# Three of the four pieces of each MLP down product as Strassen's seven half-size products, in a decoder kernel on one core

## The chip, the cores and the metric

The kernel runs on one core of a Trainium2 chip. The metric is the device time of one execution in microseconds; several runs of the same kernel are given by their median. The engines are TensorE (PE, with its weight loads as PEld), VectorE (DVE), ScalarE (ACT), GpSimd (POOL) and SyncE (SP, which issues most of the transfers).

## The reference

Two decoder blocks on 512 tokens of 1024 features, all in float32. The first block has two layers, each an attention (latent, then sliding window), a layer norm, an MLP and another layer norm; the second block is a convolution with a dilated attention, a gated feed-forward and an embedding branch. The change is in the MLPs of the first block:

```
def _mlp(x, w_up, w_down):
    h = jax.nn.relu(x @ w_up)          # [512, 1024] @ [1024, 4096]
    return (h * h) @ w_down            # [512, 4096] @ [4096, 1024]

x = _layernorm(alpha * x + _mlp(x, mlp_w_up[l], mlp_w_down[l]), ln_mlp_g[l], ln_mlp_b[l])
```

## The kernel before

A float32 product is made of three products of exact parts. `split` (L115) makes them: ScalarE casts the source to the high part, VectorE subtracts it from the source to get the low part. `mm3` (L197) then issues high x high, high x low and low x high into one accumulation. Weights come in chunks of 128 x 1024 values through `wchunk` (L151): SP loads one into a raw slot (three of them, tile names wr), and the split writes a pair of slots wh and wl, four pairs in all (pool `wp`, L53). Large tiles of 128 x 2048 values, among them the transposed activations (xth, xtl), come from thirteen slots (`bp`, L54). Eight PSUM banks of 128 x 512 hold accumulations.

Names in the rows: `wl<-wr,wh` is the low part of weights, `hh` and `hl` are the parts of the squared activations with the features on partitions, `fm`, `tm`, `tt` and `up` are banks of products, `x` is the residual stream with tokens on partitions.

`mlp_ln` (L883) is called once in each of the two layers. `up(gr)` makes 512 of the 4096 hidden features: four banks, 96 mm3 steps of three matmuls over the eight row blocks of the weights; its `ev` takes Relu on ScalarE (L896), the square on VectorE (L897) and the split. `rows(ga)` takes two groups, 1024 hidden features, for one piece of the down product. `gemm_tm` (L348) does a piece for all four token blocks and for one half of the 1024 output columns after the other, and `ev_add` (L874) adds each bank to x. The order is written out by hand:

```
            for gr in range(4):
                up(gr)
            gemm_tm(*rows(0), [LO, HI], ev_add(x, ALPHA))
            up(4), up(5)
            gemm_tm(*rows(2), [LO, HI], ev_add(x, 1.0))
            up(6), up(7)
```

After that come the third piece and the fourth, whose second column half is done token block by token block with the layer norm (`ev_add_ln`, L809). The order on each engine is set by a scheduler from the order of the program text and from priorities: `tc.high_priority(offset=...)` moves the splits of weights ahead of other work of their engine by 60 places of program order (`W_PRIO`). On the engine the instructions then run strictly in that order.

Of the kernel before, what the change touches and what calls it, by code (L numbers as in the profile page):

```python
# [37 lines left out]
# pieces of other products between the steps of an attention loop  # L38
# [6 lines left out]
MLA_WO_AT = (0, 0, 21, 23)  # the steps that the first weights of the output projection wait for  # L45
# [3 lines left out]
def tile_hybrid_decoder(ctx: ExitStack, tc: tile.TileContext, io: dict, out: bass.AP):  # L49
# [75 lines left out]
    class Ahead:  # L125
        """The first weights of the next phase, split before this one ends."""
# [5 lines left out]
        def all(self):  # L132
            """All of them, in a pool of their own."""
            p = self.stack.enter_context(pool(f"pre{n_big[0]}", 4, "right"))
            for sp in self.specs:
                self.chunks.append(wchunk(*sp[:3], p=p, gain=(sp + (None,))[3]))
            return self

        def one(self):
            """The next one, two to a pair of large slots."""  # L140
            i = len(self.chunks)
            if i % 2 == 0:
                self.slots = [big(n).rearrange("p a c -> p (a c)") for n in ("awh", "awl")]
            dst = [t[:, i % 2 * 1024:i % 2 * 1024 + 1024] for t in self.slots]
            self.chunks.append(wchunk(*self.specs[i][:3], dst=dst))
# [5 lines left out]
    def wchunk(parts, a, b, perm=None, p=None, gain=None, dst=None, prio=W_PRIO):  # L151
        """gain: the vec column of the first of the chunk's factors along the rows."""
# [50 lines left out]
    # two heads of 64 features on the halves of the partitions: of head c the first part stands on its own half,  # L203
    # the second on the other one
# [43 lines left out]
    def fm_load(W, c0, n, K, kc=None, perm=None, gain=None):  # L248
        """The k-chunks of columns c0..c0+n: a list of (k0, kn, hi, lo)."""
# [50 lines left out]
    def half_k(pb, W, X, hf):  # L300
        """One bank of features on partitions, half of the tokens; W: the weights by rows."""
# [23 lines left out]
    def parts_m(pb, chunks, X, m):  # L325
        """one_m in steps of a chunk."""
# [7 lines left out]
    def parts_t(pb, chunks, X, t):  # L334
        """one_t in steps of a chunk."""
# [52 lines left out]
    def gemm_tm_t(X, W, groups, evac, g0=0, src=None, ahead=None, nxt=None, ch=None, mid=None):  # L388
        """The same, one token block after the other with the whole of the weights at hand."""
# [26 lines left out]
    def rsqrt(v_in, n, scale, eps):  # L416
        """(scale * v_in + eps)^-1/2: with v four times the base, s = v^-1/2 and a Newton step (3 - v s^2) s."""
# [19 lines left out]
    def put_t(xt, src, t):  # L437
        """Transposes the [128 tokens, 1024] src into token block t of xt."""
# [11 lines left out]
    class Norm:  # L450
        """Layer norm of x [128, NB, D] by token blocks: the sums come with what is added to x."""
# [27 lines left out]
    def rms_norm(x, t, g, xt, xns):  # L479
        """xt block t = transpose of x * rsqrt(mean(x^2) + eps) * g."""  # L480
# [11 lines left out]
    def scale_rows(eng, a, f):  # L492
        """a times the factor f of its row."""
# [5 lines left out]
    def tri(tl, qb):  # L499
        """Columns of query block qb for the key blocks up to it, in a packed triangle."""  # L500
# [7 lines left out]
    # the T5 bias by distance, one row per token of a block, kept in DRAM for a skewed read;  # L508
    # and the vectors along the features, one column each
# [47 lines left out]
    # ================= block 1, layer 0: latent attention ==========================  # L557
# [23 lines left out]
    with ExitStack() as mla:  # L581
# [20 lines left out]
        def v_piece(h0, t):  # L602
            """Values of four heads, tokens on partitions."""
# [205 lines left out]
    def ev_add_ln(x, alpha, g, b, after):  # L809
        """x = layer_norm(alpha * x + bank) as the column halves of a token block come in."""  # L810
# [72 lines left out]
    def mlp_ln(xt_in, x, l, first, nxt, rms=False):  # L883
        """x = layer_norm(alpha * x + mlp(x)); first: the first weights; nxt() takes those of the next phase."""
# [3 lines left out]
        def up(gr):  # L888
            hh, hl = big("hh"), big("hl")
            H[gr] = [(hh[:, m, :], hl[:, m, :]) for m in range(4)]  # L890

            def ev(gi, m, pb):
                n_big[0] += 1
                r = rt.tile([P, S], F32, tag="r", name=f"r_{n_big[0]}")
                v = rt.tile([P, S], F32, tag="v", name=f"v_{n_big[0]}")
                nc.scalar.activation(r, pb, AF.Relu)  # L896
                nc.vector.tensor_tensor(out=v, in0=r, in1=r, op=ALU.mult)  # L897
                split(hh[:, m, :], hl[:, m, :], v)

            gemm_fm(xt_in[2], wu, [(gr * 512, 512)], ev, ahead=first if gr == 0 else None)  # L900
# [34 lines left out]
    # ================= block 1, layer 1: sliding window attention ==================  # L935
# [56 lines left out]
    with swa:  # L992
# [92 lines left out]
        def pair(j):  # L1085
            """Two heads of the same kv head; for c = 1 the second of them stands first."""
# [4 lines left out]
        def wo_chunk(ks, c0):  # L1091
            """The rows of two pairs of heads, as pair() has them."""
# [71 lines left out]
    def conv3(y, u, wi, nm, m, bi):  # L1164
        """y = causal depthwise convolution of u along the tokens."""
# [8 lines left out]
    # ================= block 2: convolution and dilated attention ==================  # L1174
# [5 lines left out]
    def row_sums(sq):  # L1180
        """The sums over the features of sq [128, S]: column t for the tokens of block t."""
# [99 lines left out]
    # the three dilations as one causal softmax whose weights count the branches that see a key  # L1281
# [211 lines left out]
        # embedding branch  # L1493
# [44 lines left out]
def _constants():  # L1538
    """Tables that depend on the shapes alone."""
# [47 lines left out]
```

## Time and profile before

| | us |
|---|---|
| three runs | 1753.97, 1748.44, 1754.33 |
| their median | 1753.97 |
| profiled execution, span from first to last instruction | 1746.6 |
| profiled execution, its own device time | not given beside the span |
| PE busy | 1716.4 |
| DVE busy | 924.3 |
| ACT busy | 721.0 |

The span is that of one profiled execution on the same kernel. Busy times are sums over the instructions' spans with overlap counted once. Matmuls overlap one another, so the mean duration of one in a group is longer than the time from one to the next. The two MLPs lie at about 220 to 560 us and 743 to 1072 us of the span.

### The profile page before, as it was taken

To read this page: it belongs to the slowest core of one execution; us is meant where nothing else is said; L and a number is where in the kernel's file an instruction comes from. 1 tells how busy PE (TensorE), PEld (TensorE's weight loads), DVE (VectorE), ACT (ScalarE), POOL (GpSimd) and SP (SyncE) were. 2 spreads that over 40 slices of the span, in tenths; PEclk is the share of its full clock that TensorE was granted. 3 is DMA by queue.
4 is the path that set the end of the run, shared out by engine and by line. 5 is a ranking of instruction groups with operands and counts; after the bars stand their busy time and mean duration, and the time that the engine had idled before them with its cause. 6 is when DMAs were issued, how large, how long until landed. Compare 5 with 4: busy or idle time off the path is not lost.

```text
span 1746.6 us, 21505 instructions
## 1 busy us (share of the span) xinstructions
PE 1716.4 (98%) x8431; PEld 1423.2 (81%) x8431; DVE 924.3 (53%) x1786; ACT 721.0 (41%) x1311; POOL 8.0 (0%) x10
## 2 busy tenths in 40 slices
PE   8699999999999999999999999999999999999999
PEld 8577898888888877798888888888779888888887
DVE  5576654434344678744344435755866444443454
ACT  4366433222222568534232323544864332232342
POOL 0000000000000000000000000001000000000000
PEclk9899999999999999999999999999999999999999
DMA  5712312222333223222222233132331333333221
GB/s 183 111 56 95 123 62 97 97 97 97 99 119 106 97 67 108 68 73 96 97 97 97 96 121 121 49 109 84 100 106 50 98 97 97 99 121 96 91 97 61
DMA packets 113752, 167.59 MB, mean 96 GB/s; under 512 B 9049, under 2 KB 55410, under 8 KB 113650
## 3 DMA queue, kind: packets, MB, share of 16 engines
q1 hardware_dynamic: 104736, 150.03, 26.9%
q10 hardware_dynamic: 8914, 16.18, 3.9%
q8 instruction: 66, 1.08, 0.3%
q14 instruction: 36, 0.29, 0.1%
HBM read 160.95 MB, written 5.24 MB: 95 GB/s over the span
## 4 chain that ended last, share of the span: by engine, by line
PE 93%; DVE 2%; DMA 2%; ACT 2%; ACTq 1%; issue 0%; SPq 0%; DVEq 0%
PE tm L199 9%; PE tm L201 9%; PE tm L200 9%; PE fm L200 8%; PE fm L199 8%; PE fm L201 8%; PE tt L200 3%; PE tt L201 3%; PE tt L199 3%; PE gt L200 2%; PE up L200 2%; PE up L199 2%; PE gt L201 2%; PE gt L199 2%; PE up L201 2%; PE wo L199 2%
## 5 line engine op out<-in xcount | busy, mean ns | idle before, releaser
L117 DVE TENSOR_TENSOR wl<-wr,wh 128x1024 fp32r<-128x1024 f32 (+5 forms) x283 | 301.8, 1076 | 513.4 <-ACT wh L116 512.2
L116 ACT CAST wh<-wr 128x1024 fp32r<-128x1024 f32 (+5 forms) x283 | 261.0, 933 | 572.5 <-PE tm L201 303.7
L199 PE MATMUL fm<-xth,wh 128*128 128x512 f32 (+1 forms) x640 | 235.7, 368 | 0.2 <-ACT xth L116 0.2
L200 PE MATMUL fm<-xtl,wh 128*128 128x512 f32 (+1 forms) x640 | 235.3, 368 | 0.0
L201 PE MATMUL fm<-xth,wl 128*128 128x512 f32 (+1 forms) x640 | 235.2, 367 | 0.0
L199 PE MATMUL tm<-wh,hh 128*128 128x512 f32 x448 | 174.3, 389 | 0.0
L200 PE MATMUL tm<-wl,hh 128*128 128x512 f32 x448 | 174.3, 389 | 0.0
L201 PE MATMUL tm<-wh,hl 128*128 128x512 f32 x448 | 174.3, 389 | 0.0
L199 PEld LDWEIGHTS fm<-xth,wh 128*128 128x128 f32 x640 | 120.4, 188 | 20.3 <-ACT xth L116 0.5
L201 PEld LDWEIGHTS fm<-xth,wl 128*128 128x128 f32 x640 | 120.4, 188 | 20.0
L200 PEld LDWEIGHTS fm<-xtl,wh 128*128 128x128 f32 x640 | 120.4, 188 | 19.9
L201 PEld LDWEIGHTS tm<-wh,hl 128*128 128x128 f32 x448 | 84.1, 188 | 17.5
L199 PEld LDWEIGHTS tm<-wh,hh 128*128 128x128 f32 x448 | 84.1, 188 | 17.4
L200 PEld LDWEIGHTS tm<-wl,hh 128*128 128x128 f32 x448 | 84.1, 188 | 17.4
L199 PE MATMUL gt<-xth,wh 128*128 128x512 f32 x160 | 62.3, 389 | 0.0
L200 PE MATMUL gt<-xtl,wh 128*128 128x512 f32 x160 | 62.3, 389 | 0.0
L201 PE MATMUL up<-xth,wl 128*128 128x512 f32 x160 | 62.2, 389 | 0.0
L201 PE MATMUL gt<-xth,wl 128*128 128x512 f32 x160 | 62.2, 389 | 0.0
L199 PE MATMUL up<-xth,wh 128*128 128x512 f32 x160 | 62.2, 389 | 0.0
L200 PE MATMUL up<-xtl,wh 128*128 128x512 f32 x160 | 62.2, 389 | 0.0
L199 PE MATMUL tm<-wh,ah 128*128 128x512 f32 x152 | 59.1, 389 | 0.0
L200 PE MATMUL tm<-wl,ah 128*128 128x512 f32 x152 | 59.1, 389 | 0.0
(404 smaller groups left out, 3373.7 us busy)
## 6 DMA issues: line engine op xcount, KB each, us to landing
wr<-in_mlp_w_up_dram SPq DMA_DIRECT2D x64, 512.0 KB, 3.4
wr<-in_mlp_w_down_dram SPq DMA_DIRECT2D x64, 512.0 KB, 3.8
wr<-in_w_in_dram SPq DMA_DIRECT2D x24, 512.0 KB, 5.0
wr<-in_w_gate_dram SPq DMA_DIRECT2D x22, 512.0 KB, 3.8
wr<-in_w_up_dram SPq DMA_DIRECT2D x22, 512.0 KB, 3.5
wr<-in_w_down_dram SPq DMA_DIRECT2D x22, 512.0 KB, 3.8
wr<-in_mla_w_o_dram SPq DMA_DIRECT2D x8, 512.0 KB, 3.8
wr<-in_swa_w_q_dram SPq DMA_DIRECT2D x8, 512.0 KB, 3.9
```

The source lines that it names most:

```text
L116: turned["hi"] = nc.scalar.copy(out=hi, in_=src).ins
L117: return nc.vector.tensor_tensor(out=lo, in0=src, in1=hi.bitcast(F32), op=ALU.subtract)
L199: nc.tensor.matmul(o, lhsT=sh, rhs=mh, start=start, stop=False, skip_group_check=True)
L200: nc.tensor.matmul(o, lhsT=sh, rhs=ml, start=False, stop=False, skip_group_check=True)
L201: nc.tensor.matmul(o, lhsT=sl, rhs=mh, start=False, stop=stop, skip_group_check=True)
```

## The change

Of each layer's four down pieces the first three become one level of Strassen's scheme in Winograd's form. With A the 512 tokens x 1024 hidden features of a piece, cut in halves of 256 tokens and 512 features, and B its 1024 x 1024 weights, cut in halves of 512 rows and 512 columns, seven products of half size replace the eight. Their operands are sums and differences of the quarters, made on VectorE in place, before the split in high and low parts. A product has four row blocks, two token blocks and 512 columns: 24 matmuls. Three pairs of banks (R1, R2, R3, tile names r) take part of the products on top of each other, and each state of a pair is added to one or more quarters of x: 18 adds of 128 x 512 for a piece where there were 8.

The squared activations of these pieces are not split as they come; they are kept in float32 in two large tiles (hr), and the square is done on ScalarE. The weights of B are loaded whole, four blocks of 512 x 512 in slots of 1 MB of their own (pool `mb`, names wq); their splits go through the same four pairs wh and wl. The operands of A (names aop, high and low part in one tile) come from the thirteen large slots. The up products go in pairs of banks (256 features) instead of four. `WEAVE` sets the order of the seven steps (-1) and of the four up pairs (0 to 3) of the next two groups within a piece. The last piece and the layer norm stay as they were; other lines of the diff only lose comments.

```diff
+WEAVE = (-1, -1, -1, 0, -1, 1, -1, -1, 2, -1, 3)
+A_PRIO, B_PRIO = 120, 80
...
+        def squared(put):
+            def ev(m, pb):
...
                 nc.scalar.activation(r, pb, AF.Relu)
-                nc.vector.tensor_tensor(out=v, in0=r, in1=r, op=ALU.mult)
-                split(hh[:, m, :], hl[:, m, :], v)
-
-            gemm_fm(xt_in[2], wu, [(gr * 512, 512)], ev, ahead=first if gr == 0 else None)
+                put(m, r)
+            return ev
+
+        def put_raw(raw):
+            return lambda m, r: nc.scalar.activation(raw[:, m, :], r, AF.Square)
...
+        def down_steps(c, alpha):
...
+            for r, h in ((0, 0), (1, 1), (0, 1), (1, 0)):
+                B[r, h] = q = mb.tile([P, 4, S], F32, tag="q", name=f"wq_{n_big[0]}")
+                for i in range(2):
+                    nc.sync.dma_start(out=q[:, 2 * i:2 * i + 2, :],
+                                      in_=krows(wd, c * 8 + r * 4 + 2 * i, 2, h * 512, 512))
...
+            def product(R, a, b, start):
+                for i, (wh, wl) in enumerate(b):
+                    for tb in range(2):
+                        for k in range(2):
+                            ts_ = slice(tb * P, (tb + 1) * P)
+                            kk = 2 * i + k
+                            mm3(R[tb], (a[:, 0, kk, ts_], a[:, 1, kk, ts_]), (wh[:, k, :], wl[:, k, :]),
+                                start and kk == 0, kk == 3)
...
+            a22 = a_op(A22)
+            a_sum(A22, A22, A21, ALU.subtract)
+            s2 = a_op(A22)
+            b_sum(B11, B12, B11, ALU.add)
+            b = b_op(B11)
+            R2 = banks2("r")
+            product(R2, s2, b, True)
+            add(R2, 1, 0)
+            yield
+            a12 = a_op(A12)
+            b = b_op(B21)
+            product(R1, a12, b, False)
+            add(R1, 0, 0, alpha)
+            yield
...
+            a_sum(A12, A12, A22, ALU.subtract)
+            s4 = a_op(A12)
+            b = b_op(B22)
+            product(R2, s4, b, False)
+            add(R2, 0, 1)
+            yield
...
-            for gr in range(4):
-                up(gr)
-            gemm_tm(*rows(0), [LO, HI], ev_add(x, ALPHA))
-            up(4), up(5)
-            gemm_tm(*rows(2), [LO, HI], ev_add(x, 1.0))
-            up(6), up(7)
+            with pool("mb", 4) as mb:
...
+                for c in range(3):
+                    ds = down_steps(c, ALPHA if c == 0 else 1.0)
+                    for what in WEAVE:
+                        if what < 0:
+                            next(ds)
+                            continue
+                        gr, half = 2 * c + 2 + what // 2, what % 2
...
+                        up_pair(gr, half, ev)
-        gemm_tm(*rows(4), [LO, HI], ev_add(x, 1.0))
```

In the change's order the first place is VectorE between the third and the fourth of the seven steps, in the second piece of the first layer. Before, in a down piece, VectorE had splits of weights and runs of four adds:

```order
L117 TENSOR_TENSOR wl_537_3213<-wr_537_3211,wh_537_3212 128x1024
L877 SCALAR_TENSOR_TENSOR x1_375_1795<-x1_375_1795,tm_523_3019 128x512
L877 SCALAR_TENSOR_TENSOR x1_375_1795<-x1_375_1795,tm_524_3020 128x512
L877 SCALAR_TENSOR_TENSOR x1_375_1795<-x1_375_1795,tm_525_3021 128x512
L877 SCALAR_TENSOR_TENSOR x1_375_1795<-x1_375_1795,tm_526_3022 128x512
L117 TENSOR_TENSOR wl_538_3243<-wr_538_3241,wh_538_3242 128x1024
L117 TENSOR_TENSOR wl_545_3283<-wr_545_3281,wh_545_3282 128x1024
```

Now, at that place (aop_577 is the operand A12 of the fourth step, wl_582 the weights of the up pair after it, r_568 and r_569 the banks of the third step):

```order
L120 TENSOR_TENSOR wl_578_3478<-wq_553_3272,wh_578_3477 128x1024
L880 SCALAR_TENSOR_TENSOR x1_375_1795<-x1_375_1795,r_568_3377 128x512
L120 TENSOR_TENSOR wl_579_3482<-wq_553_3272,wh_579_3481 128x1024
L880 SCALAR_TENSOR_TENSOR x1_375_1795<-x1_375_1795,r_569_3378 128x512
L950 TENSOR_TENSOR hr_513_2838<-hr_513_2838,hr_534_3088 128x4x256
L956 TENSOR_TENSOR wq_553_3272<-wq_553_3272,wq_550_3263 128x1024 x2
L956 TENSOR_TENSOR wq_550_3263<-wq_551_3266,wq_550_3263 128x1024 x2
L120 TENSOR_TENSOR wl_582_3515<-wr_582_3513,wh_582_3514 128x1024
L120 TENSOR_TENSOR aop_577_3474<-hr_534_3088,aop_577_3474 128x1024
L120 TENSOR_TENSOR aop_586_3580<-hr_513_2838,aop_586_3580 128x1024
```

Five wide sums and a split of up weights stand ahead of the low part of A12 that the fourth step reads.

The second place is ScalarE at the same step. Before, in a down piece, it had casts of weights only:

```order
L116 CAST wh_535_3152<-wr_535_3151 128x1024
L116 CAST wh_536_3182<-wr_536_3181 128x1024
L116 CAST wh_537_3212<-wr_537_3211 128x1024
L116 CAST wh_538_3242<-wr_538_3241 128x1024
L116 CAST wh_545_3282<-wr_545_3281 128x1024
```

Now, with up_571 and up_572 the two banks of the up pair before the fourth step:

```order
L119 CAST wh_582_3514<-wr_582_3513 128x1024
L896 ACTIVATE r_575_3468<-up_571_3406 128x512
L901 ACTIVATE hr_570_3405<-r_575_3468 128x512
L119 CAST aop_577_3474<-hr_534_3088 128x1024
L119 CAST aop_586_3580<-hr_513_2838 128x1024
L119 CAST wh_583_3544<-wr_583_3543 128x1024
L896 ACTIVATE r_576_3471<-up_572_3407 128x512
```

The cast of A12 stands behind the Relu and the square of the up pair's first bank.

The third place is VectorE in the layer norm that ends the second layer's attention, just ahead of the second MLP (names nm, rv, rr, ra, ro are 128x1 values of the norm, gb its gain and bias). Before:

```order
L460 SCALAR_TENSOR_TENSOR x1_375_1795,sum_943_6396<-x1_375_1795,tt_944_6398 128x512
L423 SCALAR_TENSOR_TENSOR ra_940_6375<-rv_937_6372,rs_939_6374 128x1
L427 SCALAR_TENSOR_TENSOR ro_941_6376<-ra_940_6375,rs_939_6374 128x1
L466 TENSOR_SCALAR nm_945_6412<-sum_943_6396 128x1
L472 SCALAR_TENSOR_TENSOR x1_375_1795<-x1_375_1795,ro_941_6376,gb_926_6330 128x1024
L470 SCALAR_TENSOR_TENSOR x1_375_1795<-x1_375_1795,nm_945_6412,gb_926_6330 128x1024
```

Now:

```order
L463 SCALAR_TENSOR_TENSOR x1_375_1795,sum_982_6425<-x1_375_1795,tt_983_6427 128x512
L426 SCALAR_TENSOR_TENSOR ra_979_6404<-rv_976_6401,rs_978_6403 128x1
L956 TENSOR_TENSOR wq_1043_6961<-wq_1042_6958,wq_1043_6961 128x1024
L430 SCALAR_TENSOR_TENSOR ro_980_6405<-ra_979_6404,rs_978_6403 128x1
L469 TENSOR_SCALAR nm_984_6441<-sum_982_6425 128x1
L475 SCALAR_TENSOR_TENSOR x1_375_1795<-x1_375_1795,ro_980_6405,gb_965_6359 128x1024
L463 SCALAR_TENSOR_TENSOR x1_375_1795,sum_992_6470<-x1_375_1795,tt_991_6457 128x512
L473 SCALAR_TENSOR_TENSOR x1_375_1795<-x1_375_1795,nm_984_6441,gb_965_6359 128x1024
L422 TENSOR_SCALAR rv_986_6446<-ss_985_6442 128x1
L956 TENSOR_TENSOR wq_1043_6961<-wq_1042_6958,wq_1043_6961 128x1024
```

The two sums B22 - B12 of the first piece have moved into the norm, one between two of its small steps of the first token block, one within those of the second.

## Rows read from the trace of the kernel before

**Rows 1.** The page, its head and part 1: busy us, share, instructions.
```profile
span 1746.6 us, 21505 instructions
...
PE 1716.4 (98%) x8431; PEld 1423.2 (81%) x8431; DVE 924.3 (53%) x1786; ACT 721.0 (41%) x1311; POOL 8.0 (0%) x10
```
**Rows 2.** The page, part 4: the chain that ended last, by engine.
```profile
PE 93%; DVE 2%; DMA 2%; ACT 2%; ACTq 1%; issue 0%; SPq 0%; DVEq 0%
```
**Rows 3.** Windows 220:312, 312:560, 760:850, 850:1072: busy us; clock, DMA share, GB/s.
```profile
312.00:560.00 248.00, 248.00 (x1096) 205.43 (x1095) 100.38 (x120) 70.82 (x86) 0.00 (x0) 1.00 0.32 105
...
sum 652.00, PE 651.76 PEld 545.15 DVE 272.41 ACT 201.47 POOL 0.00; mean PE 162.94 PEld 136.29 DVE 68.10 ACT 50.37 POOL 0.00
```
**Rows 4.** Timeline of PE, from a down product into an up product: start, duration.
```profile
429.63 0.39 PE L201 MATMUL tm<-wh,hl 128*128 128x512 f32 x1
...
443.45 0.39 PE L199 MATMUL fm<-xth,wh 128*128 128x512 f32 x1
```
**Rows 5.** Groups by line and shape: count, busy us, mean ns of one, idle before.
```profile
L117 DVE TENSOR_TENSOR wl<-wr,wh 128x1024 fp32r<-128x1024 f32 x205 | 250.0, 1225 | 489.0 <-ACT wh L116 488.1
L116 ACT CAST wh<-wr 128x1024 fp32r<-128x1024 f32 x205 | 214.5, 1053 | 539.2 <-PE tm L201 300.0 <-PE fm L200 155.7 <-PE gt L200 39.2
...
L199 PE MATMUL tm<-wh,hh 128*128 128x512 f32 x448 | 174.3, 389 | 0.0
...
L897 DVE TENSOR_TENSOR v<-r 128x512 f32<-128x512 f32 x64 | 43.9, 689 | 6.8 <-ACT r L896 6.1
...
L896 ACT ACTIVATE r<-fm 128x512 f32<-128x512 f32 x64 | 37.9, 595 | 19.0 <-PE fm L201 19.0
...
L877 DVE SCALAR_TENSOR_TENSOR x<-x,tm 128x512 f32<-128x512 f32 x48 | 31.8, 684 | 14.9 <-PE tm L201 14.9
...
L470 DVE SCALAR_TENSOR_TENSOR x<-x,nm,gb 128x1024 f32<-128x1024 f32 x16 | 20.5, 1284 | 10.1 <-ACT sq L469 10.1
```
**Rows 6.** Timeline of DVE at the end of the first up groups.
```profile
314.02 1.23 DVE L117 TENSOR_TENSOR wl<-wr,wh 128x1024 fp32r<-128x1024 f32 x1 [0.26 <-ACT wh L116]
315.16 0.69 DVE L117 TENSOR_TENSOR hl<-v,hh 128x512 fp32r<-128x512 f32 x1
...
331.64 1.28 DVE L877 SCALAR_TENSOR_TENSOR x<-x,tm 128x512 f32<-128x512 f32 x2
```
**Rows 7.** Timelines of ACT and of DVE: a handoff, and casts back to back.
```profile
253.03 1.05 ACT L116 CAST wh<-wr 128x1024 fp32r<-128x1024 f32 x1 [3.22 <-PE fm L200]
...
254.12 1.23 DVE L117 TENSOR_TENSOR wl<-wr,wh 128x1024 fp32r<-128x1024 f32 x1 [3.58 <-ACT wh L116]
...
269.42 1.05 ACT L116 CAST wh<-wr 128x1024 fp32r<-128x1024 f32 x1
270.37 0.61 ACT L116 CAST hh<-v 128x512 fp32r<-128x512 f32 x1
```
**Rows 8.** ACT: Squares of the sq tiles (min/median/max ns); table loads, first and last.
```profile
L1209 ACT ACTIVATE sq<-tt x4: 578/597/598, 1102.7 to 1133.6; 128x512 f32<-128x512 f32 x4
...
L421 ACT ACT_TABLE_LOAD x5 | 6.4, 1283 | 0.1
...
L1513 ACT ACT_TABLE_LOAD x1 | 1.3, 1283 | 0.0
```
**Rows 9.** DMA issues (KB each, us to landing), and the window 756:760.
```profile
wr<-in_mlp_w_down_dram SPq DMA_DIRECT2D x64, 512.0 KB, 3.8
...
756.00:760.00 4.00, 4.00 (x36) 4.00 (x35) 1.23 (x1) 1.59 (x2) 0.00 (x0) 1.00 0.91 290
```
**Rows 10.** Timeline at the entry of the second MLP.
```profile
719.80 1.23 DVE L117 TENSOR_TENSOR wl<-wr,wh 128x1024 fp32r<-128x1024 f32 x1 [0.18 <-ACT wh L116]
...
730.21 0.22 DVE L423 SCALAR_TENSOR_TENSOR ra<-rv,rs 128x1 f32<-128x1 f32 x1
...
741.59 1.28 DVE L472 SCALAR_TENSOR_TENSOR x<-x,ro,gb 128x1024 f32<-128x1024 f32 x1
...
742.93 1.09 PE L444 MATMUL pt<-ident,x 128*128 128x128 f32 x8
```

More of the change, by code (lines that the diff above doesn't have):

```diff
@@ new lines, in put_raw, with put_split, put, up_pair @@
+        def put_raw(raw):
+            return lambda m, r: nc.scalar.activation(raw[:, m, :], r, AF.Square)
+        def put_split(hh, hl):
+            def put(m, r):
+                nc.scalar.activation(r, r, AF.Square)
+                split(hh[:, m, :], hl[:, m, :], r)
+            return put
+        def up_pair(gr, half, ev):
+            banks = [bank("up") for _ in range(2)]
+            for k0 in (0, 4):
+                wh, wl = wchunk(krows(wu, k0, 4, gr * 512 + half * 256, 256), 4, 256)
+                for k, m in ([(k, m) for k in range(4) for m in range(2)] if k0 == 0 else
+                             [(k, m) for m in range(2) for k in range(4)]):
+                    cs = slice(m * P, (m + 1) * P)
+                    mm3(banks[m], (wh[:, k, cs], wl[:, k, cs]), xt_in[2][k0 + k], k0 + k == 0, k0 + k == 7)
+                tick()
+            for m in range(2):
+                ev(half * 2 + m, banks[m])
@@ L902, in rows, with a_op, a_sum, b_sum @@
         def rows(ga):
             return H.pop(ga) + H.pop(ga + 1), wd[ga * 512:(ga + 2) * 512, :]
-        with pool("rt", 2) as rt:
-            for gr in range(4):
-                up(gr)
-            gemm_tm(*rows(0), [LO, HI], ev_add(x, ALPHA))
-            up(4), up(5)
-            gemm_tm(*rows(2), [LO, HI], ev_add(x, 1.0))
-            up(6), up(7)
+        ts2 = slice(0, 256), slice(256, 512)
+        def down_steps(c, alpha):
+            ra, rb = RAW.pop(2 * c), RAW.pop(2 * c + 1)
+            A11, A21, A12, A22 = ra[:, :, ts2[0]], ra[:, :, ts2[1]], rb[:, :, ts2[0]], rb[:, :, ts2[1]]
+            B = {}
+            for r, h in ((0, 0), (1, 1), (0, 1), (1, 0)):
+                n_big[0] += 1
+                B[r, h] = q = mb.tile([P, 4, S], F32, tag="q", name=f"wq_{n_big[0]}")
+                for i in range(2):
+                    nc.sync.dma_start(out=q[:, 2 * i:2 * i + 2, :],
+                                      in_=krows(wd, c * 8 + r * 4 + 2 * i, 2, h * 512, 512))
+            B11, B12, B21, B22 = B[0, 0], B[0, 1], B[1, 0], B[1, 1]
+            def a_op(src):
+                o = big("aop")
+                hl = o.rearrange("p k c -> p (k c)").rearrange("p (f k c) -> p f k c", f=2, k=4)
+                with tc.high_priority(offset=A_PRIO):
+                    split(hl[:, 0], hl[:, 1], src)
+                return hl
+            def a_sum(out, a, b, op):
+                with tc.high_priority(offset=A_PRIO):
+                    nc.vector.tensor_tensor(out=out, in0=a, in1=b, op=op)
+            def b_sum(out, a, b, op):
+                with tc.high_priority(offset=A_PRIO):
+                    for i in range(2):
+                        ks = slice(2 * i, 2 * i + 2)
+                        nc.vector.tensor_tensor(out=out[:, ks, :], in0=a[:, ks, :], in1=b[:, ks, :], op=op)
+            def b_op(src):
+                res = []
+                for i in range(2):
+                    n_big[0] += 1
+                    wh = wp.tile([P, 1024], F32R, tag="wh", name=f"wh_{n_big[0]}")
+                    wl = wp.tile([P, 1024], F32R, tag="wl", name=f"wl_{n_big[0]}")
+                    with tc.high_priority(offset=B_PRIO):
+                        split(wh, wl, src[:, 2 * i:2 * i + 2, :].rearrange("p k c -> p (k c)"))
+                    res.append([t.rearrange("p (k c) -> p k c", k=2) for t in (wh, wl)])
+                return res
+            def product(R, a, b, start):
[6 more added lines that the diff above has]
+                                start and kk == 0, kk == 3)
+            def add(R, th, h, al=1.0):
+                for tb in range(2):
+                    ev_add(x, al)(h, 2 * th + tb, R[tb])
+            def banks2(n):
+                return [bank(n) for _ in range(2)]
+            a11 = a_op(A11)
+            b = b_op(B11)
+            R1 = banks2("r")
+            product(R1, a11, b, True)
+            for th, h in ((0, 1), (1, 0), (1, 1)):
+                add(R1, th, h, alpha)
+            yield
+            a_sum(A21, A11, A21, ALU.subtract)
+            s3 = a_op(A21)
+            b_sum(B12, B22, B12, ALU.subtract)
+            b = b_op(B12)
+            R3 = banks2("r")
+            product(R3, s3, b, True)
+            add(R3, 1, 1)
+            yield
[3 more added lines that the diff above has]
+            b_sum(B11, B12, B11, ALU.add)
+            b = b_op(B11)
+            R2 = banks2("r")
[6 more added lines that the diff above has]
+            add(R1, 0, 0, alpha)
+            yield
+            a_sum(A11, A11, A22, ALU.add)
+            s1 = a_op(A11)
+            b_sum(B21, B21, B11, ALU.subtract)
+            b_sum(B11, B22, B11, ALU.subtract)
+            b = b_op(B11)
+            product(R2, s1, b, False)
+            add(R2, 1, 1)
+            yield
+            b = b_op(B21)
+            product(R3, a22, b, False)
+            add(R3, 1, 0)
+            yield
+            a_sum(A12, A12, A22, ALU.subtract)
[3 more added lines that the diff above has]
+            add(R2, 0, 1)
+            yield
@@ new lines, in mlp_ln @@
+        with pool("rt", 2) as rt:
+            RAW = {}
+            RAW[0], RAW[1] = big("hr", F32), big("hr", F32)
+            ev = squared(put_raw(RAW[0]))
+            gemm_fm(xt_in[2], wu, [(0, 512)], lambda gi, m, pb: ev(m, pb), ahead=first)
+            with pool("mb", 4) as mb:
+                for half in range(2):
+                    up_pair(1, half, squared(put_raw(RAW[1])))
+                for c in range(3):
[5 more added lines that the diff above has]
+                        gr, half = 2 * c + 2 + what // 2, what % 2
+                        if half == 0 and c < 2:
+                            RAW[gr] = big("hr", F32)
+                            ev = squared(put_raw(RAW[gr]))
+                        elif half == 0:
+                            hh, hl = big("hh"), big("hl")
+                            H[gr] = [(hh[:, m, :], hl[:, m, :]) for m in range(4)]
+                            ev = squared(put_split(hh, hl))
+                        up_pair(gr, half, ev)
+                    for _ in ds:
+                        pass
```

5 lines of the change are left out of this document (removed).

## Prediction

> **What bounds the kernel now.** I read the page from the top: the span and the busy shares [rows 1], then the chain that ended last [rows 2]. TensorE is busy for 98% of the span and carries 93% of the chain, VectorE and ScalarE carry 2% each. Then the stretches: both MLPs are 652 us of the 1746.6, and in the windows that cover them TensorE is busy for 651.8 us, at a granted clock of 1.00, with VectorE busy for 41% (100.4 of 248 us) and ScalarE for 29% [rows 3]. So in the MLPs a matmul less is time less, as long as the other engines deliver on time.
>
> What a matmul is worth is not its duration. A product with the weights shows 389 ns in the groups [rows 5], but in the timeline the next one starts after 0.2266 us: from 429.63 to 443.45 us lie 61 steps, 13.82 / 61 [rows 4].
>
> **The change, part by part.**
>
> *Matmuls.* One piece of a down product is 8 rows of weights x 4 token blocks x 2 column halves x 3 = 192 matmuls. Seven products of half size are 7 x 4 x 2 x 3 = 168. Three pieces in each of two layers: 6 x 24 = 144 matmuls less. The order has 143 rows less on TensorE, and the up products keep their number. 144 x 0.2266 = **-32.6 us**. By the 389 ns it would be -56 us; the pitch decides. I write S1 to S7 for the seven products (24 matmuls, 5.44 us each), U0 to U3 for the four up pairs woven in (48 matmuls, 10.88 us each). A piece with its ups takes 87.0 us now and 81.6 us then.
>
> *VectorE.* Before, a piece with two up groups needs 16 wide splits (128x1024, 1225 ns), 8 squares and 8 narrow splits (689 ns, both 128x512) and 8 adds (684 ns) [rows 5]: 19.6 + 16.5 = 36.1 us of 87.0. After: 8 splits of up weights, 14 of B, 7 of A, 4 sums of A and 8 of B, 41 wide ones, and 18 adds: 50.2 + 12.3 = 62.5 us of 81.6. The sums have no row of their own; the nearest are the wide subtraction at 1225 and, in place, L470 at 1284 ns [rows 5]. I take 1225; with 1284 the twelve sums cost 0.7 us more per piece. VectorE stays below TensorE over a piece, so what counts is whether a stretch of it is late.
>
> *ScalarE.* 29 wide casts (1053 ns), 8 Relu (595) and 8 squares (597, the 128x512 Square of another stage [rows 8]): 40.1 us of 81.6, before 26.6 of 87.0. The trace has seven groups of table loads, from L421 to L1513 by their busy time [rows 8], none at a line with a Relu or a Square, so none is added.
>
> *The tight place: S1, S2, S3, U0, then S4.* VectorE is in order. The split of a chunk of weights waits for a slot of a ring of four, so the last split for S2 can start on ScalarE only when U3 has ended, which is when S1 starts (call it 0). Then the low part of A22 waits for Relu, square and cast of the last up bank: the cast of the weights lets the next start after 0.95 us (269.42 to 270.37 [rows 7]), then Relu 0.60, square 0.60, cast 1.05 and handoffs of 0.04 (253.03 + 1.05 to 254.12 [rows 7]), 3.3 us. From 3.35 us VectorE has 16 wide operations and 10 adds in line up to the low part of A12, which S4 needs. Back to back, a wide one lets the next start after 1.14 us (314.02 to 315.16), an add after 0.60 (1.28 for two) [rows 6]. I take 0.61 for the adds: 16 x 1.14 + 10 x 0.61 + 0.1 for the last one's tail = 24.4, so the operand is there at 27.8 us. TensorE needs it after 120 matmuls, 27.2 us, and four more of S4 that need only the high part: 28.1. ScalarE's chain there ends at the same time: the second half of an up pair goes bank by bank, so U0's first bank is done 12 matmuls, 2.72 us, before U0 ends, at 24.5; Relu, square, cast (0.60, 0.60, 1.05) and the subtraction (1.23) with four handoffs of 0.04 give 28.1. There is no reserve at all, so I price S4 at **0.4 us** a piece; the ends are 0 and 2.6 (below, first rival, with the extra narrow split of the last piece).
>
> *S7.* Its operand A12 - A22 is cast behind the Relu and the square of U2's first bank: 0.60 + 0.60 + 1.05 + 1.23 and four handoffs, 3.6 us, against 2.72 + 0.9 = 3.6. I take **0.2 us**, ends 0 and 0.5. S1 to S3, S5 and S6 have their operands 0.7 us or more ahead. Together 6 x 0.6 = **+3.6 us**.
>
> *Loads.* 8 loads of 512 KB a piece as before, same bytes, now into four slots of 1 MB. SP waits for such a slot with the loads of up weights queued behind it: B12 of the next piece is issued after S6's split, and the two up chunks behind it are needed some 20 us later, with 3.8 us to landing [rows 9]. VectorE's first sum of B12 stands between S5's adds and the splits for U2 and waits for the landing; U2's second chunk can be 7 us late before TensorE sees it. I cost this at nothing; the cover is that slack. POOL has no part.
>
> *Entry of the second layer.* Two sums of B12 (2 x 1.14 us) now stand in VectorE's queue inside the layer norm that ends the attention. There the transposes of the third token block start at 742.93, right after VectorE's last step at 741.59 + 1.28 [rows 10]: no reserve. They also wait for loads behind an up chunk whose raw slot is freed by the split at 719.80, so SP issues them from about 721.0 on; 2.5 MB at the 290 GB/s of [rows 9] take 8.6 us, which is 729.6 or a little later, and VectorE comes to the first sum after the step at 730.21 [rows 10]. I take the 2.3 us of the sums less a little idle time, **+2.0 us**; ends 0 and, with loads 4 us late, 6. The first layer has no such sums there, since its buffers are still in use.
>
> **Sum**: -32.6 + 3.6 + 2.0 = -27.0 us on a span of 1746.6. The page has no time of that execution beside its span; the three timed runs lie 1.8 to 7.7 us above the span, their median, 1753.97, by 7.4. Forecast: 1753.97 - 27.0 = **1727 us**.
>
> [...] In the timeline a wide operation on VectorE starts the next one 0.09 us before its own end: 1.23 us long at 314.02, followed at 315.16 [rows 6]. [...]
>
> **Rivals.**
> 1. *VectorE pays full durations in the tight place.* If each of those operations takes its whole 1.23 or 0.69 us, the operand is there at 3.35 + 16 x 1.23 + 10 x 0.69 = 29.9 us (30.6 in the last piece), 1.8 us late in four pieces and 2.5 in two, together 12.2 us; with 0.5 for S7 and 2.0 at the entry -32.6 + 12.2 + 3 + 2 = -15.4, so 1739. For it: many of the operations are chained or wait for ScalarE, and every such handoff costs 0.04 us. Against it: the pitches of [rows 6]. [...]
> 2. *The savings are eaten, no change.* S4 late by 4 us a piece, or S1 to S3 late too because the ring of four slots allows a lead of two products only, and 6 us at the entry: -32.6 + 24 + 6 = -2.6, about 1751. For it: no reserve at S4. Against it: S1, S2, S3, S5 and S6 come out in time by the same sums.
> 3. *VectorE becomes the bound of S1 to S4, and it is slower than before.* Place: the 26 operations from A22 to A12's low part. If they take r times their pitch, they end at 3.35 + 24.4 r; at r = 1.3 (a wide one at 1.48 us) that is 35.1, 7.0 us late, 42 us in six pieces: -32.6 + 42 + 1.2 + 2 = +12.6, so 1767. It decides from r = 1.2 on (4.9 us a piece). For it: sums in place, with operands that are strided halves of a tile, which the trace of before doesn't have at this width. Against it: in place 1284 ns against 1225 is r = 1.05 [rows 5].
>
> **Chances.** Forecast 0.60, rival 1 0.24, rival 2 0.10, rival 3 0.06. A measurement of this kernel can tell about 0.5% from no change, 8.8 us: faster means below 1745.2, slower above 1762.7. The forecast and rival 1 lie below: faster 0.84, same 0.10, slower 0.06. Range: without any stall 1753.97 - 32.6 = 1721.4, and the fastest run of before lies 5.5 us under the median, so 1716 at the low end; at the high end it takes in rival 1 with its entry at 4 us, 1740. That leaves out rivals 2 and 3 and a little of rival 1.
>
> **What would show it.** Right: products on the r tiles with a pitch of 0.2266 us, 1008 of them; in the windows of the MLPs TensorE idle for under 6 us in all, with S4's third matmul kind (the low part of A against the high part of B) as the place of the waits, on the subtraction that writes aop; VectorE at some 75% there. Wrong: idle TensorE of 2 us or more before every S4 (rival 1), waits before wl tiles of S1 to S3 (rival 2), wide sums of over 1.3 us each (rival 3), or a wait of more than 4 us for the transposes at the entry of the second layer. The forecast also fails if a woven product has another pitch than the plain one.

## The result and the profile after

| | before | after |
|---|---|---|
| median of four runs, us | 1753.46 | 1719.41 |
| the runs | 1753.97, 1748.44, 1754.33, 1752.95 | 1722.70, 1718.35, 1719.61, 1719.22 |
| span of the profiled execution | 1746.6 | 1720.9 |
| its own time | 1748.44 | 1722.70 |

The ratio is 0.9823, with a 95% interval of 0.9808 to 0.9839. The runs of before, of after and of most kernels here lie in a lower or an upper group, some 3 to 6 us apart by the length of the program's opening (last section): lower against lower, 1748.44 to the mean of three, 1719.06, the change is worth 29.4 us, upper against upper, 1753.75 to 1722.70, 31.1. The two profiled executions differ in their opening and can't be subtracted as a whole.

So the accounting goes by stages. This is the timeline of TensorE at the four borders of the MLPs: the first matmul of the first up group (an fm bank), and the first of the last piece's second column half (a tt bank), in both layers. Between the two lies all that the change touches. Columns: start, duration, engine, line, operation, what it writes and reads. Before:

```profile
223.27 0.38 PE L199 MATMUL fm<-xth,wh 128*128 128x256 f32 x1 [0.24 <-ACT xth L116]
...
552.25 0.39 PE L199 MATMUL tt<-wh,hh 128*128 128x512 f32 x1
...
742.45 0.39 PE L199 MATMUL fm<-xth,awh 128*128 128x256 f32 x1 [0.24 <-ACT xth L116]
...
1072.57 0.39 PE L199 MATMUL tt<-wh,hh 128*128 128x512 f32 x1
```

After:

```profile
227.41 0.38 PE L202 MATMUL fm<-xth,wh 128*128 128x256 f32 x1 [0.24 <-ACT xth L119]
...
541.35 0.39 PE L202 MATMUL tt<-wh,hh 128*128 128x512 f32 x1
...
731.53 0.38 PE L202 MATMUL fm<-xth,awh 128*128 128x256 f32 x1 [0.24 <-ACT xth L119]
...
1047.18 0.39 PE L202 MATMUL tt<-wh,hh 128*128 128x512 f32 x1
```

The first MLP went from 328.98 to 313.94 us, the second from 330.12 to 315.65: -15.04 and -14.47, together **-29.5**. The stretch between the two MLPs is 190.20 and 190.18, and from the last border to the end of the span it is 674.03 and 673.72, so outside the MLPs and the opening only 0.3 us moved. The 4.1 us that after starts later belong to the opening.

72 matmuls are gone in each layer, 72 x 0.2266 = 16.32 us. The woven products keep that pitch: S5 and S6 of the second piece, 48 matmuls, lie from 399.40 to 410.28, 0.2267 us each. So 1.28 us was lost in the first layer and 1.85 in the second. The page of after, its head, the busy row and the chain, stands against [rows 1, 2]:

```profile
span 1720.9 us, 21349 instructions
...
PE 1691.0 (98%) x8287; PEld 1399.3 (81%) x8287; DVE 1052.7 (61%) x1884; ACT 811.2 (47%) x1405; POOL 8.0 (0%) x10
...
PE 94%; DVE 2%; ACT 1%; DMA 1%; ACTq 1%; issue 0%; SPq 0%
```

TensorE is as much the bound as before; VectorE's share rose to 61% of the span, ScalarE's to 47%. Windows of the woven stretch, against [rows 3]; the columns are window, its length, then busy time and instructions of PE, PEld, DVE, ACT and POOL, the granted clock, DMA share and GB/s:

```profile
260.00:550.00 290.00, 290.00 (x1276) 238.64 (x1275) 193.76 (x205) 137.25 (x162) 0.00 (x0) 1.00 0.30 97
...
382.00:464.00 82.00, 82.00 (x361) 67.36 (x360) 58.22 (x60) 38.92 (x46) 0.00 (x0) 1.00 0.29 90
464.00:545.00 81.00, 81.00 (x358) 66.70 (x357) 42.63 (x50) 37.34 (x46) 0.00 (x0) 1.00 0.32 104
```

In a piece (382 to 464) VectorE is busy for 58.2 of 82 us, 71%, and TensorE all the time. The groups of the new work, against [rows 5, 8, 9]; duration of one in ns behind the busy time, then the engine's idle time ahead and what ended it:

```profile
L120 DVE TENSOR_TENSOR wl<-wq,wh 128x1024 fp32r<-128x1024 f32 x84 | 102.6, 1221 | 88.6 <-ACT wh L119 88.6
...
L204 PE MATMUL r<-wh,aop 128*128 128x512 f32 x336 | 130.1, 393 | 0.0
L204 PEld LDWEIGHTS r<-wh,aop 128*128 128x128 f32 x336 | 63.1, 188 | 16.3 <-DVE aop L120 3.3
...
L880 DVE SCALAR_TENSOR_TENSOR x<-x,r 128x512 f32<-128x512 f32 x108 | 69.3, 680 | 0.0
L120 DVE TENSOR_TENSOR aop<-hr,aop 128x1024 fp32r<-128x1024 f32 x42 | 50.4, 1222 | 24.0 <-ACT aop L119 24.0
...
wq<-in_mlp_w_down_dram SPq DMA_DIRECT2D x48, 512.0 KB, 4.6
```

The products on the r tiles are 3 x 336 = 1008 matmuls. The only wait of note in the weave is the one named ahead: the third kind of matmul of S4, and of S7 too, on the subtraction that writes aop. The row of the weight loads (PEld) shows it, 3.3 us in all; the rows of the matmuls don't, since the ones before, 0.39 us long and 0.23 apart, are still running then. The tight place of the second piece, ScalarE, then VectorE, then TensorE, with idle time and releaser in brackets:

```profile
380.32 0.60 ACT L896 ACTIVATE r<-up 128x512 f32<-128x512 f32 x1 [1.89 <-PE up L204]
380.95 0.64 ACT L901 ACTIVATE hr<-r 128x512 f32<-128x512 f32 x1
381.49 1.98 ACT L119 CAST aop<-hr 128x1024 fp32r<-128x1024 f32 x2
```

```profile
376.28 4.62 DVE L956 TENSOR_TENSOR wq<-wq,wq 128x1024 f32<-128x1024 f32 x4
380.83 1.22 DVE L120 TENSOR_TENSOR wl<-wr,wh 128x1024 fp32r<-128x1024 f32 x1
382.56 2.36 DVE L120 TENSOR_TENSOR aop<-hr,aop 128x1024 fp32r<-128x1024 f32 x2 [0.52 <-ACT aop L119]
```

```profile
382.84 0.39 PE L202 MATMUL r<-wh,aop 128*128 128x512 f32 x1
...
383.52 0.39 PE L203 MATMUL r<-wl,aop 128*128 128x512 f32 x1
383.84 0.50 PE L204 MATMUL r<-wh,aop 128*128 128x512 f32 x1
384.17 0.39 PE L202 MATMUL r<-wh,aop 128*128 128x512 f32 x1
...
388.52 0.39 PE L202 MATMUL up<-xth,wh 128*128 128x512 f32 x1
```

The low part (382.56, the first of two) comes 0.09 us too late for L204, and the next step is 0.10 late. All 24 matmuls of S4 take 5.68 us (382.84 to 388.52) instead of 5.44, so S4 loses 0.24 here. Measured in this way, S4 loses 0.24 to 0.27 us in the first two pieces of the first layer and nothing in the third, S7 0.26 in all three; together that is the 1.28 us. VectorE had been idle for 0.52 us: ScalarE's chain of Relu, square and cast came last here, not VectorE's line of 26 operations.

### The profile page after: what moved, and what is told of

It reads as the page before. It is cut to its first block, busy times and chain, and to the rows that moved or that the text cites. A ratio compares the mean times of both kernels' runs of the same rounds, so it can differ in the third digit from the quotient of the medians.

```text
span 1720.9 us, 21349 instructions
## 1 busy us (share of the span) xinstructions
PE 1691.0 (98%) x8287; PEld 1399.3 (81%) x8287; DVE 1052.7 (61%) x1884; ACT 811.2 (47%) x1405; POOL 8.0 (0%) x10
## 4 chain that ended last, share of the span: by engine, by line
PE 94%; DVE 2%; ACT 1%; DMA 1%; ACTq 1%; issue 0%; SPq 0%
PE up L202 8%; PE up L203 8%; PE up L204 8%; PE r L204 5%; PE r L202 4%; PE r L203 4%; PE tm L202 4%; PE tm L204 4%; PE tm L203 4%; PE tt L203 3%; PE tt L204 3%; PE tt L202 3%; PE fm L202 2%; PE fm L203 2%; PE fm L204 2%; PE gt L203 2%
## 5 line engine op out<-in xcount | busy, mean ns | idle before, releaser
L203 PE MATMUL up<-xtl,wh 128*128 128x512 f32 x608 | 236.5, 389 | 0.0
L202 PE MATMUL up<-xth,wh 128*128 128x512 f32 x608 | 236.5, 389 | 0.0
L204 PE MATMUL up<-xth,wl 128*128 128x512 f32 x608 | 236.2, 389 | 0.0
L120 DVE TENSOR_TENSOR wl<-wq,wh 128x1024 fp32r<-128x1024 f32 x84 | 102.6, 1221 | 88.6 <-ACT wh L119 88.6
L204 PEld LDWEIGHTS up<-xth,wl 128*128 128x128 f32 x608 | 114.1, 188 | 23.8
L202 PEld LDWEIGHTS up<-xth,wh 128*128 128x128 f32 x608 | 114.1, 188 | 23.7
L203 PEld LDWEIGHTS up<-xtl,wh 128*128 128x128 f32 x608 | 114.1, 188 | 23.5
L202 PE MATMUL r<-wh,aop 128*128 128x512 f32 x336 | 130.9, 390 | 0.0
L203 PE MATMUL r<-wl,aop 128*128 128x512 f32 x336 | 130.9, 390 | 0.0
L204 PE MATMUL r<-wh,aop 128*128 128x512 f32 x336 | 130.1, 393 | 0.0
L204 PEld LDWEIGHTS r<-wh,aop 128*128 128x128 f32 x336 | 63.1, 188 | 16.3 <-DVE aop L120 3.3
L202 PEld LDWEIGHTS r<-wh,aop 128*128 128x128 f32 x336 | 63.1, 188 | 13.2 <-ACT aop L119 0.4
L204 PE MATMUL gt<-xth,wl 128*128 128x512 f32 x160 | 62.2, 389 | 0.0
```

The lines of the kernel that those rows point to most:

```text
L120: return nc.vector.tensor_tensor(out=lo, in0=src, in1=hi.bitcast(F32), op=ALU.subtract)
L202: nc.tensor.matmul(o, lhsT=sh, rhs=mh, start=start, stop=False, skip_group_check=True)
L203: nc.tensor.matmul(o, lhsT=sh, rhs=ml, start=False, stop=False, skip_group_check=True)
L204: nc.tensor.matmul(o, lhsT=sl, rhs=mh, start=False, stop=stop, skip_group_check=True)
```

## The experiments

The times of the MLPs in the table are the stretches between the borders above, read from each trace. The medians contain openings of different length; the stretches do not, and in the second execution of after they come out within 0.1 us of the first. The pinned kernels are another matter (below).

| kernel | first MLP | second MLP | median, us |
|---|---|---|---|
| before | 328.98 | 330.12 | 1753.46 |
| e2, before, square on ScalarE | 328.98 | 330.12 | 1749.53 |
| e1, woven, plain products | 328.99 | 330.10 | 1749.28 |
| e6, second layer plain | 313.86 | 330.11 | 1734.53 |
| after | 313.94 | 315.65 | 1719.41 |
| after, once more | 313.85 | 315.70 | 1719.75 |
| e3, square back on VectorE | 313.61 | 315.57 | 1720.50 |
| e4, operand once more | 313.86 | 315.55 | 1720.63 |
| e7, entry sums later | 313.85 | 314.94 | 1717.45 |
| e8, pinned | 315.43 | 317.29 | 1722.15 |
| e4p, pinned, once more | 323.79 | 325.51 | 1741.01 |
| e5p, pinned, three times | 339.94 | 342.13 | 1771.87 |
| e9, ups begun early | 312.66 | 313.79 | 1718.47 |

**Is it the matmuls, or what came with them?** e1 keeps the weave, the whole-block loads and the square on ScalarE, and takes Strassen out:

```diff
-            a_sum(A21, A11, A21, ALU.subtract)
...
+            for h, (Bt, Bb) in enumerate(((B11, B21), (B12, B22))):
+                b = b_op(Bt)
+                R0, R1 = banks2("r"), banks2("r")
+                product(R0, a11, b, True)
...
+                product(R1, a21, b, True)
...
+                b = b_op(Bb)
+                product(R0, ac[0], b, False)
+                add(R0, 0, h, alpha)
...
+                product(R1, ac[1], b, False)
+                add(R1, 1, h, alpha)
```

> The changed kernel with the same weave, the same loads of whole blocks, float32 squares on ScalarE, but eight plain half products in a piece instead of Strassen's seven: no sums of A or B, 8 adds to x instead of 18, 24 matmuls more in each of six pieces. Theory (the gain is the matmuls that are gone, at their pitch): 144 x 0.2266 = 32.6 us come back, less some 3 us of waits at S4, S7 and the entry of the second layer, so about 1749 us, within 0.3% of the kernel before. Rival (the weave, the loads or ScalarE's squares bring a good part of the gain): it stays below 1738.

Measured: 1749.28, ratio to before 0.9988 (0.9977 to 1.0000). Its MLPs take what those of before take, to 0.02 us. The weave and the loads bring nothing by themselves. e2 has the other edit alone, the square on ScalarE in the kernel before:

```diff
-                nc.vector.tensor_tensor(out=v, in0=r, in1=r, op=ALU.mult)
+                nc.scalar.activation(v, r, AF.Square)
```

> The kernel before with one edit: the square of the MLP goes from VectorE to ScalarE. Theory: TensorE bounds the MLPs and VectorE is 41% busy there, so 0 us, within 0.3% of the kernel before (1753). Rival (the square's place is part of the gain by itself): 3 us or more faster.

Measured: ratio 0.9996 (0.9983 to 1.0009), the same MLPs to 0.01 us. e6 uses e1's products in the second layer alone (`if l == 1:`):

> The changed kernel with plain half products in the second layer alone, Strassen in the first. Theory: 3 x 24 x 0.2266 = 16.3 us come back, less about 1 us of waits in that layer's weave and 0.9 at its entry (the sums there are gone): +14.4, about 1734, and the trace shows the whole difference inside the second MLP. Rival (the gain is not in proportion to the pieces): under +9 or over +20.

Measured: 1734.53, ratio 0.9905 (0.9883 to 0.9926), and the whole difference to after lies in the second MLP, +14.46 us. The gain goes with the matmuls, layer by layer.

**How much room do the other engines have?** e3 gives VectorE its squares back, 8 of 128x512 a piece:

```diff
-            return lambda m, r: nc.scalar.activation(raw[:, m, :], r, AF.Square)
+            return lambda m, r: nc.vector.tensor_tensor(out=raw[:, m, :], in0=r, in1=r, op=ALU.mult)
```

> The changed kernel with the MLP's squares back on VectorE: 8 more 128x512 operations for it in each of six pieces, 8 fewer for ScalarE. Theory (only the deadline of S4's operand counts, VectorE's other work has spare time, and the order of the program lets U1's first matmuls run ahead): in the tight place stand one square and one split more, 0.6 + 1.14 us, against 0.5 us that VectorE had spare and some 11 matmuls of U1 (2.5 us) that the order now puts ahead of S4's low part; so 0 to +5 us, 1719 to 1725. Rival (VectorE has no time left, its whole extra work is on the path): 6 x 8 x 0.6 = 29 us, 1748.

```profile
L901 DVE TENSOR_TENSOR hr<-r x48: 675/686/694, 240.5 to 941.5; 128x512 f32<-128x512 f32 x48
```

These 48 squares at 0.686 us (min/median/max in ns in the row), and 16 more in the last pieces, cost nothing: the MLPs are 0.1 to 0.3 us shorter than in after. VectorE has time to spare; the scheduler answered a later operand by putting some of U1's matmuls ahead of S4's low part (eleven in the first piece). Moving the square to ScalarE was not needed for the gain. e4 makes S4's operand itself late, by computing its low part twice:

```diff
                 with tc.high_priority(offset=A_PRIO):
                     split(hl[:, 0], hl[:, 1], src)
+                    for _ in range(again):
+                        nc.vector.tensor_tensor(out=hl[:, 1], in0=src, in1=hl[:, 0].bitcast(F32), op=ALU.subtract)
...
-            a12 = a_op(A12)
+            a12 = a_op(A12, 1)
```

> The changed kernel; the low part of A12, S4's operand, is computed a second time into the same place, one wide VectorE operation more in each of six pieces, on the path of S4. The order on TensorE is left to the scheduler, which now puts ten matmuls of U1 (2.27 us) ahead of S4's low part in all six pieces. Theory (no reserve at S4, but other matmuls can fill the time): 1.14 us later, in four pieces 2.28 with S5's split between the two, covered by 2.27 us: 0 to +2 us in all. Rival (a late operand at S4 is paid in full): +7 us or more.

Measured: 1720.63, and the same MLPs as after. The ten matmuls that the scheduler moved cover the whole delay. So e4p forbids that: every matmul of an up pair is issued behind the last product (`tc.issue_after`); e5p does the same with `a_op(A12, 3)`, and e8 pins without computing anything twice.

> The same second computation of A12's low part, with the order on TensorE pinned: no matmul of U1 may stand ahead of S4's last one. Theory (no reserve at S4): each piece waits for 1.14 us, or 2.28 where S5's split stands between the two, less 0 to 0.5 us spare: +5 to +11 us, and the trace shows the waits at the third kind of S4's matmuls. Rival (the operand has over 1 us of reserve): 0 to +2 us.

> As the run before it, pinned, but A12's low part is computed three more times. Theory: two more wide operations at their pitch in each of six pieces, 6 x 2 x 1.14 = 13.7 us over the run before; if VectorE pays full durations 6 x 2 x 1.22 = 14.6. [...]

> The changed kernel with the order on TensorE pinned as in the two pinned runs, and nothing computed twice: the control for them. Only in the third piece of each layer does the order move, by five matmuls of U1 and three of U3. Theory (the pinning itself costs little; the repeated operand and what follows it cost the 20 us): S4 of the two third pieces waits some 0.7 us, so 0 to +3 us, 1719 to 1723. Rival (the pinning costs a good part of the 20 us): 1727 or more.

Measured: the pinning costs 1.5 and 1.6 us (e8 against after), at S4 and at S7 of the third pieces, some 0.8 us at each; the expectation had S4 alone. In the traced executions, the one extra operation costs 8.4 and 8.2 us more (e4p against e8), the two further ones another 32.8 in both layers (e5p against e4p). The ratios to before are 0.9956 (0.9937 to 0.9975) for e4p and 1.0127 (1.0110 to 1.0144) for e5p: a chain that is late enough at this one place does make the kernel slower than before. Both missed their expectation, the second by a factor of more than two (32.8 us against 13.7). A small part of it shows on VectorE: where a repeated subtraction stands right behind one that writes the same place, and where the sum behind it overwrites what it reads, the next one starts 1.26 us after the last, not 1.13, as VectorE of e5p shows in the first piece:

```profile
300.41 1.22 DVE L120 TENSOR_TENSOR wl<-wr,wh 128x1024 fp32r<-128x1024 f32 x1
301.54 2.48 DVE L951 TENSOR_TENSOR aop<-hr,aop 128x1024 fp32r<-128x1024 f32 x2
304.06 1.23 DVE L956 TENSOR_TENSOR hr<-hr 128x1024 f32<-128x1024 f32 x1
```

The first of the two starts 1.13 us after a subtraction that it does not depend on, the second 1.26 after the first (2.48 - 1.22), the sum another 1.26 later. That is 0.13 us a pair, against a miss of 19 us. The waits of TensorE of e4p in the first MLP (us in total, times, longest), and windows around the one in the second piece:

```profile
PE r L204 <- DVE aop L951: 6.7, 3, 2.3
```

```profile
382.00:385.20 3.20, 1.00 (x6) 0.50 (x4) 3.20 (x4) 2.62 (x4) 0.00 (x0) 1.00 0.55 164
385.20:388.60 3.40, 3.40 (x8) 2.72 (x9) 2.21 (x2) 0.00 (x0) 0.00 (x0) 0.50 0.25 65
388.60:392.00 3.40, 3.40 (x16) 2.80 (x16) 2.02 (x3) 1.42 (x2) 0.00 (x0) 1.00 0.25 89
```

Two things had been left out. The split of S5's operand stands between the two computations in every piece, not in four of six, so each of the six waits is that of two operations (2.4 to 2.5 us more than a step). And in one piece of each layer the granted clock fell to 0.50 right after the wait: 8 matmuls in 3.4 us instead of 16. In e5p the waits are 5.9 to 6.5 us (other operations stand between the repeated ones) and slower matmuls followed all six: behind the wait that ends at 1017.54 us one started every 0.43 us up to 1022.40, instead of every 0.23, and the mean granted clock of the execution is 0.984, against 0.993 in e4p.

One operation more on S4's path thus cost 2.8 us a piece ((8.4 + 8.2) / 6), not 1.14, when nothing may fill the wait. That is the traced execution, 1739.24 us, near the low end of e4p's ten runs (1737.89 to 1752.83). The longest has a mean granted clock of 0.985 against 0.993; over 1745 us the difference is worth some 14 us (an estimate from these rounded clocks), about what it is longer. So the price of such waits changes from run to run.

**The entry of the second layer.** e7 lets the first sums run only behind the last split of the transposes:

```diff
+                    if c == 0 and l == 1:
+                        es.enter_context(tc.issue_after(turned[3]))
```

> The changed kernel; the two sums of B12 for the first piece of the second layer may stand on VectorE only behind the last split of the layer's transposes, not inside the layer norm ahead of it. Theory (the sums cost 0.8 us at the entry): TensorE's extra wait of about 1.1 us ahead of the transposes of the third token block falls back to 0.4 or less, and the time to 1718 to 1719, which the timed runs can not tell from no change. Rival (something else is late there): the wait stays.

TensorE's waits in the window 725 to 1050, first of after, then of e7:

```profile
PE pt L447 <- DVE x L475: 0.9, 1, 0.9
PE fm L202 <- ACT xth L119: 0.2, 1, 0.2
```

```profile
PE fm L202 <- ACT xth L119: 0.2, 1, 0.2
```

The wait on the layer norm's last step is gone and the second MLP is 0.71 us shorter. Its four runs (1717.21 to 1718.12, a little under what was expected) lie some 1.5 us under the mean of after's three lower ones; with the opening moving runs by more, that alone would show nothing.

**A version without the waits.** e9 is e7 with the up pairs U1 and U3 as generators that emit their first three mm3 steps (nine matmuls) one place earlier. An up pair has 16 such steps, 48 matmuls; a whole up group is 32 steps with 96 matmuls, not the 96 steps named in the section on the kernel before. The places:

```diff
-WEAVE = (-1, -1, -1, 0, -1, 1, -1, -1, 2, -1, 3)
+WEAVE = (-1, -1, -1, 0, 1, -1, 1, -1, -1, 2, 3, -1, 3)
+EARLY = (1, 3)
```

> The changed kernel with the entry sums behind the transposes and with the first nine matmuls of U1 put ahead of S4 and those of U3 ahead of S7, which gives each operand 2.04 us more. Theory: the ten or so waits of 0.2 us at S4 and S7 go (1.8 us) and 0.7 us at the entry: 1716 to 1718. Rival (the split of U1's weights now takes a slot of the ring and a place on VectorE ahead of S4's): new waits ahead of S4's weights, 1719 or more.

> The changed kernel once more, as the partner of the two runs beside it: 1718 to 1723 us.

The borders of e9 (its lines are one higher):

```profile
228.63 0.38 PE L203 MATMUL fm<-xth,wh 128*128 128x256 f32 x1 [0.24 <-ACT xth L120]
...
541.29 0.39 PE L203 MATMUL tt<-wh,hh 128*128 128x512 f32 x1
...
731.55 0.38 PE L203 MATMUL fm<-xth,awh 128*128 128x256 f32 x1 [0.24 <-ACT xth L120]
...
1045.34 0.39 PE L203 MATMUL tt<-wh,hh 128*128 128x512 f32 x1
```

312.66 and 313.79 us: the MLPs of before less 16.32 are 312.66 and 313.80. Every matmul that Strassen takes away is now time, with no wait left beyond those of before. Measured by runs, 1718.47 (1715.74 to 1721.13) against 1719.75 for after beside it (1719.36 to 1722.67): the 3.1 us that the stages show is below what these runs can tell, since the opening moves them by more. By its median e9 missed both the 1716 to 1718 expected and the rival's 1719; the trace, which shows no new wait, decides against the rival.

## Why the prediction was right

*Matmuls, -32.6.* Shown: e1 and e6 give back what was gained, e9 has the whole of it to 0.01 us. The pitch, not the 389 ns of the group, was the price.

*S4 and S7, +3.6.* Right place, a third too dear: 1.28 us in the first layer and 1.85 - 0.71 = 1.14 in the second, 2.4 together. The arrival was forecast almost exactly: S1 of the second piece starts at 355.64, so the low part of A12, done at 382.56 + 1.22 = 383.78, is there 28.1 us after it, and needed at 28.1. VectorE's line would have ended at 27.6, where I had 27.8, so the chain of ScalarE was the last one. The prices beside it were guesses: 0.4 a piece for S4, measured 0.25 in four pieces and nothing in the two third ones, and 0.2 for S7, measured 0.26 in each of the three pieces of the first layer. In the third pieces, where I had expected VectorE to be later still, the order on TensorE has five matmuls of U1 ahead of S4's low part and three of U3 ahead of S7's. e8, without that help, loses 1.5 us a layer more. That the order is made with the lateness in view was no part of my sum.

*Squares.* Taken at 597 ns, they take 632 on ScalarE. The 35 ns more are part of the lateness of its chain at S4.

*VectorE.* 50.2 + 12.3 us were costed for a piece, 58.2 were measured busy (overlap counted once), 71% where I had 75%.

*Loads, 0.* 4.6 us to landing, no wait on these loads in the MLPs: right.

*Entry, +2.0.* It was 0.7. The first sum started at 719.41, straight behind the step before it at 719.28, so the loads were there, and 0.7 of the sums' 2.3 us reached TensorE. The rest went into idle time of VectorE that I had put at "a little": in before it waits for 0.17, 0.27, 0.77 and 0.27 us between its steps at 729.59 and 741.59, 1.5 in all, and in after, between the same steps (718.67 and 731.52), not at all.

*Rival 1* (full durations) is refuted: four sums in a row take 4.62 us, (4.62 - 1.22) / 3 = 1.13 from one to the next, although the third overwrites what the first read. An operation that stood right behind one on which it depends started later, after 1.26 us (e5p), where the prediction had 1.14 for every pair. *Rivals 2 and 3* had the place, but not the delay: S4 lost 0.27 us at most, not 4 or 7, and the wide sums take 1.22 us, not 1.48. Their prices also assumed a fixed order. With the free order one more operation costs nothing (e4); with a pinned one it costs its delay and, after two of the six waits, a granted clock of 0.50 too (e4p).

The sum was -27.0 where the stages show -29.5. The other 5 us between 1727 and 1719.4 are the base: I started from 1753.97, a run of the upper group, and the median of after is of the lower one. The run that was profiled took 1748.44; from there the same sum ends at 1721.4. As it was, the measured 1719.41 lies below even the figure that I had for no stall at all, 1721.4 too, and inside the range only by the 5.5 us taken off for a faster run of before. How many of the four runs of each kernel fall in which group was luck.

## What to carry to other kernels

In these MLPs TensorE was busy throughout at a steady pitch (0.2266 us), and removed instructions times that pitch was the gain where no operand came late (to 0.01 us of 16.32 in e9), so the work was to find the one deadline that had no reserve. Filling that deadline with other ready work of the bounding engine (nine matmuls here) took the wait away; making the late chain faster was not tried. Compare stages between fixed borders when the total moves by more than the effect.

## What the hardware showed that was not expected

The opening has a stretch at a granted clock of 0.50 whose length differs between executions of one kernel: in windows of 2 us the clock is 0.50 from 90 to 102 us in after, from 90 to 94 in after once more, and from 88 to 92 in before. It begins with a wait of TensorE for VectorE of 6.2 us (after), 6.4 (after once more) and 6.8 (before). The same window, 96 to 104 us, of before, of after, and of after once more:

```profile
96.00:104.00 8.00, 8.00 (x41) 6.22 (x40) 6.75 (x26) 5.27 (x14) 0.00 (x0) 1.00 0.30 83
```

```profile
96.00:104.00 8.00, 8.00 (x27) 6.33 (x27) 5.30 (x20) 3.47 (x10) 0.00 (x0) 0.61 0.30 83
```

```profile
96.00:104.00 8.00, 8.00 (x40) 6.27 (x41) 7.41 (x25) 5.62 (x15) 0.00 (x0) 1.00 0.32 83
```

Where the clock stays low here (0.61 in the mean, 27 matmuls instead of 40), the first up product starts at 227.41 us instead of 224.44, and that is nearly all of what parts these two executions of after (1722.70 and 1719.64). Of the other runs only the mean clock is on record, and there too the longer ones have the lower one (0.993 against 0.995 in before). What decides how long the stretch is stays open.

The second is the price of a wait: in e4p six waits of nearly the same length (2.4 to 2.5 us) were followed by a granted clock of 0.50 twice, once in each layer, at 1.7 us a time (3.4 us at 0.50); in e5p all six waits, of 5.9 us and more, were followed by slower matmuls. Why two of six and not the others stays open.
